# Hybrid decoder layer on one core: the first attention head's tensors loaded during the projections, the last down product's splits issued ahead of evictions, and the last output block computed in two halves

## Chip, cores and metric

The kernel runs on one core of one Trainium2 chip. The metric is the device time of one execution in microseconds. The kernel before was run three times; its time is the median of these runs. One further execution was recorded by the hardware profiler, and all durations quoted from a profile come from that one.

## The reference

The kernel computes one layer of a hybrid decoder for a sequence of 1024 tokens of width 1024, with 16 learned meta tokens put in front. All tensors are float32. Cut to what matters:

```python
h = concat([meta, x])                                  # 1040 x 1024
proj = rmsnorm(h, attn_norm_w) @ w_in                   # one projection, split by columns
o_gdn = gated_deltanet_group(...)                       # 4 heads of 128: short conv, chunked delta rule
# forgetting attention, 8 heads of 64, queries in blocks of 128, c = cumsum(log f):
sc = q[s:e] @ k[:e].T * scale + c[s:e, None] - c[None, :e]
p = softmax(where(causal, sc, MASK_VALUE))
o_fox = p @ v[:e]
h = h + concat([o_gdn, o_fox]) @ w_out
h = h + (silu(u @ w_gate) * (u @ w_up)) @ w_down        # u = rmsnorm(h, ffn_norm_w), d_ff = 2816
out = rmsnorm(h, final_norm_w)[16:]
```

## The kernel before

**Precision.** Every large product runs as three products of rounded operands: an operand is split into a high part (a cast by ScalarE, line 158) and a low part (a subtraction by VectorE, line 159), and high x high, high x low and low x high are summed in PSUM. The helper is `split` (line 157).

**Stages.** The layer is one long program: norm and projections; the delta-rule group's preparation and its scan over eight chunks of 128 tokens; attention over eight heads; the output projection; the feed-forward part; a final norm.

**The order on TensorE is written out by hand.** A small planner, `PeOrder` (line 43), keeps a modelled clock `od.t`. Chains of work are generators that yield the time at which their next step is due; whenever no chain is due, the planner takes the next matmul of a "fill". While the scan's chain runs (`scan`, line 692, one `chunk` of line 719 after another), the fill is `fox` (line 823): the attention group's projections, in the order v, k, q. `fox_proj` (line 672) works on blocks of 128 output columns, m = 0 to 3, in three chunks of some 342 to 348 tokens; each chunk's result is split into `fhl` (lines 687 and 688) and written to HBM (`q_d`, `k_d`, line 690). Afterwards the chain is `attention` (line 995), due `ATT0` = 9.0 modelled microseconds later (line 1077), and the fill is the delta-rule group's half of the output projection, `wout_gdn` (line 1057, tiles `wog`); six of its sixteen tiles are kept back for the stretch behind attention.

**The other engines and the DMA queue.** All DMAs named here are issued by SyncE (SP), in one queue. The order on VectorE, ScalarE, GpSimdE and SP is not written out: the framework's scheduler arranges it from the order of the program and a model of the times, and may move a load far ahead of its place in the program once the memory that it fills is free. `tc.issue_after(ins)` keeps instructions made inside it behind `ins` where they go to the same engine.

**The scan** loads for each chunk 1.75 MB in four DMAs (`ra`, `rb`, `rc`, `zt`, lines 722 to 728, two buffers each).

**Attention.** `att_head(h)` (line 885) issues eight DMAs for head h: `cr` (the cumulative gate, broadcast to 128 partitions), `sa` in two halves (q, high and low), `kk` in two halves (k, high and low), `vt` (v), and `vmt` twice (v of the meta tokens). Its tiles lie in the pool `al` (line 875), which is opened after the scan's pool `sp` is closed and so lies in memory that the scan used; each tag has two buffers, one for even and one for odd heads. Head 1's loads are kept behind the last write of `q_d` (line 1002). `scores` (line 903) makes two matmuls into one of two PSUM banks (lines 927 and 928), and VectorE adds the bias `bi` and takes a running minimum (line 930); ScalarE takes the exponential (line 935). `values` (line 950) transposes the probabilities and multiplies by v.

**The down product** comes as seven products p1, p6, p2, p7, p5, p4, p3 of half-sized blocks (`PH2`, line 1378), each of 11 operand pairs, in order of time. `down_ops` (line 1354) loads and splits a product's operands in three chunks of 4, 4 and 3 pairs; the three sets of buffers (`SETS`) are used in turn, so a product's third chunk takes the buffers of the third chunk of the product before. Each product but the last runs over four token blocks t inside each pair; the last, p3, runs block by block (line 1446), 33 matmuls of 512 columns each. `evict` (line 1414) adds a product from PSUM to its target; for p4 and p3 it then calls `final(u)` (line 1398), which for every block but 3 squares a row, takes the inverse root (line 205, on GpSimdE), multiplies (line 1040) and writes 512 KB to the output. The program has the operands' splits for the next product ahead of the evictions; the scheduler is free to mix them. For block 3, the last, `final` works in halves of 512 columns (lines 1404 to 1412).

Of the kernel before, what the change touches and what calls it, by code (L numbers as in the profile page):

```python
# [21 lines left out]
NT = S // P  # L22
GH = 4
FH = 8
DH = 64
DFF = 2816
NFF = DFF // P
EPS = 1e-6
# [3 lines left out]
GRP = 4  # L32
LV0 = (76.0, 119.0)
LAT = 0.4
ATT0 = 9.0
LEAD = 0.6
CO = 3.0
RES = 6
# [57 lines left out]
def tile_hymba_layer(ctx, tc, x, meta, attn_norm_w, w_in, conv_w, a_log, dt_bias, gdn_norm_w,  # L96
                     fgate_b, w_out, ffn_norm_w, w_gate, w_up, w_down, final_norm_w, out):
    nc = tc.nc
    x, out, w_in, conv_w = x[0], out[0], w_in[0], conv_w[0]
# [36 lines left out]
    mhalf = const.tile([P, 32], F32, name="mhalf")  # L136
# [10 lines left out]
    q_d = dram.tile([4, 2, P, S], F32, name="q_d")  # L147
# [6 lines left out]
    wraw = wrc.enter_context(tc.tile_pool(name="wraw", bufs=2, side="right"))  # L154
    wsp = wrc.enter_context(tc.tile_pool(name="wsp", bufs=4, side="right"))

    def split(dst_hi, dst_lo, src):
        cast = nc.scalar.copy(dst_hi, src)  # L158
        nc.vector.tensor_sub(dst_lo, src, dst_hi.bitcast(F32))  # L159
        return cast  # L160

    def load_w(parts, name):
# [40 lines left out]
    def inv_rms(dst, ssq, n, scale, tmp):  # L203
        nc.vector.tensor_scalar(tmp, ssq, scale, EPS, op0=ALU.mult, op1=ALU.add)
        nc.gpsimd.tensor_tensor(dst, tmp, mhalf[:tmp.shape[0], :n], op=ALU.pow)
# [12 lines left out]
    pre = ExitStack()  # L218
# [441 lines left out]
                                          w[1][k][:, :n]) for k in range(KT)], n / 2400)  # L660

    last = [None]

    fox_ws = [(GZ, 256, "z0"), (FV + 256, 264, "fv1"), (FV, 256, "fv0"), (FK, 256, "fk0"), (FK + 256, 256, "fk1"),
              (FQ, 256, "fq0"), (FQ + 256, 256, "fq1")]
# [6 lines left out]
    def fox_proj(dst, chunks, off, scale, nm):  # L672
        for b in range(2):
            w = fox_w.pop(0)
            for i in range(2):
                m = 2 * b + i
                for ci, (c0, n) in enumerate(chunks):
                    if (i, ci) == (0, 1):
                        fox_load()
                    acc = ps_mm(f"pj_{nm}{m}_{c0}")  # L680
                    yield from mm3g(acc[:, :n], [(w[0][k][:, P * i:P * i + P], w[1][k][:, P * i:P * i + P],
                                                  uh[:, k, c0:c0 + n], ul[:, k, c0:c0 + n])
                                                 for k in range(KT)], n / 2400)
                    od.on("act", n / 1200)
                    od.on("dve", n / 900)
                    hl = fp.tile([P, 2, 348], F32R, tag="fhl", name=f"fhl_{nm}{m}_{c0}")
                    nc.scalar.activation(hl[:, 0, :n], acc[:, :n], AF.Copy, scale=scale)
                    nc.vector.scalar_tensor_tensor(hl[:, 1, :n], acc[:, :n], scale, hl[:, 0, :n].bitcast(F32),
                                                   op0=ALU.mult, op1=ALU.subtract)
                    last[0] = nc.sync.dma_start(dst(m)[:, :, c0 - off:c0 - off + n], hl[:, :, :n].bitcast(F32))  # L690

    def scan():
        yield from meta_state()
# [168 lines left out]
    ogp = ogc.enter_context(tc.tile_pool(name="og", bufs=1))  # L862
    ogh = ogp.tile([P, GH, S], F32R, name="ogh")
    ogl = ogp.tile([P, GH, S], F32R, name="ogl")
    sp = scc.enter_context(tc.tile_pool(name="sp", bufs=1))
    cp = scc.enter_context(tc.tile_pool(name="cp", bufs=1, side="right"))
    od.add(scan(), od.t + 4.0, front=True)
# [4 lines left out]
    uctx.close()  # L872

    alc = ExitStack()
    al_ = alc.enter_context(tc.tile_pool(name="al", bufs=1))
    atc = ExitStack()
    ap_ = atc.enter_context(tc.tile_pool(name="ap", bufs=1, side="right"))
    ap2 = atc.enter_context(tc.tile_pool(name="ap2", bufs=1, side="right"))
    rsum = ap_.tile([P, FH, NT], F32, name="rsum")
    phm = ap2.tile([48, 512], F32R, name="phm")  # L880
    vmts = [al_.tile([48, P], F32R, name=f"vmt{i}") for i in range(2)]
    for z in [phm] + vmts:
        nc.gpsimd.memset(z.bitcast(F32), 0.0)

    def att_head(h):
        m, hb = h // 2, h % 2
        rows = slice(DH * hb, DH * hb + DH)
        kk = al_.tile([P, 2, T], F32R, tag="kk", bufs=2, name=f"kk_{h}")
        sa = al_.tile([P, S], F32R, tag="sa", bufs=2, name=f"sa_{h}")
        cr = al_.tile([P, T], F32, tag="cr", bufs=2, name=f"cr_{h}")  # L890
        nc.sync.dma_start(cr, c_d[h].partition_broadcast(P))
        for i in range(2):
            half = slice(DH * i, DH * i + DH)
            nc.sync.dma_start(sa[half].bitcast(F32), q_d[m, i, rows])
            nc.sync.dma_start(kk[half].bitcast(F32), k_d[m, rows])
        vt = al_.tile([P, NT, P], F32R, tag="vt", bufs=2, name=f"avt_{h}")
        nc.sync.dma_start(vt.bitcast(F32), v_d[h, NM:T].rearrange("(t p) d -> p t d", p=P))
        vmt = vmts[h % 2]
        for r in (0, 32):
            nc.sync.dma_start(vmt[r:r + NM].bitcast(F32), v_d[h, 0:NM])  # L900
        return m, rows, kk, sa, cr, vt, vmt

    def scores(h, g, hd, out):
        m, rows, kk, sa, cr, vt, vmt = hd
# [89 lines left out]

    def attention():
        groups = [(h, g) for h in range(FH) for g in range(NT // GRP)]
        hds, ptl, pos = {}, {}, [0.0]

        def score_stream():
            for i, (h, g) in enumerate(groups):  # L1000
                if h not in hds:
                    with tc.issue_after(last[0].ins) if h == 1 else nullcontext():
                        hds[h] = att_head(h)
                ptl[i] = []
                for n, rdy in enumerate(scores(h, g, hds[h], ptl[i])):
                    pos[0] = i + n / (5, 9)[g]
                    yield rdy
            pos[0] = 1e9

        ss = score_stream()  # L1010

        def ahead(x):
            while pos[0] < x:
                r = next(ss, None)
                if r is None:
                    return
                yield r

        yield from ahead(1.0)
        rot[0] = 0  # L1020
        for i, (h, g) in enumerate(groups):
            nt = GRP * (g + 1) + 1
            yield from ahead(i + 1.0)
            for k, rdy in enumerate(values(h, g, hds[h], ptl[i])):
                yield from ahead(i + 1.0 + LEAD + k / (2 * nt))
                yield rdy
        yield from av_step(0)
        rot[0] = 1
# [97 lines left out]
    rot[0] = 1  # L1126
    wo0c.close()
    alc.close()
    ogc.close()
    akc.close()  # L1130
    gplc.close()
# [179 lines left out]
    with tc.manual_schedule(engines={mybir.EngineType.PE}):  # L1311
# [76 lines left out]
        fnw = f3.tile([P, D], F32, name="fnw")  # L1388
        nc.sync.dma_start(fnw, final_norm_w.partition_broadcast(P))

        def down3(dst, op, t, first, i, cont):
            f, (ah, al), (wh, wl) = op
            c = slice(P * t, P * t + P)
            for n, (a, b) in enumerate(((ah, wh), (ah, wl), (al, wh))):
                nc.tensor.matmul(dst, a[:, f, c], b[:, f], start=(first and i == 0 and n == 0),  # L1395
                                 stop=(i == NF - 1 and n == 2), skip_group_check=cont)

        def final(t):
            y = f3.tile([P, D], F32, tag="y", bufs=3, name=f"y_{t}")
            if t != 3:  # L1400
                norm2(hs[t], fnw, y, f3, f"o{t}")
                nc.sync.dma_start(out[P * t:P * t + P], y)
                return
            sst = f3.tile([P, 6], F32, name="sst")
            halves = [lo_, hi_]
            for i, c in enumerate(halves):
                nc.scalar.activation(y[:, c], hs[t][:, c], AF.Square, accum_out=sst[:, i:i + 1])
            V.tensor_add(sst[:, 2:3], sst[:, 0:1], sst[:, 1:2])
            inv_rms(sst[:, 4:5], sst[:, 2:3], 1, 1.0 / D, sst[:, 3:4])
            for c in halves:  # L1410
                V.scalar_tensor_tensor(y[:, c], hs[t][:, c], sst[:, 4:5], fnw[:, c], op0=ALU.mult, op1=ALU.mult)
                nc.sync.dma_start(out[P * t:P * t + P, c], y[:, c])

        def evict(p, bk, t):
            u = t + 4
# [21 lines left out]
        for n, p in enumerate(PH2):  # L1437
            s = "y" if p in ("p6", "p7", "p4") else "x"
            first = p in ("p1", "p6", "p5", "p4")
            if first:  # L1440
                if s == "x":
                    sets[s] = [ps_s(f"x{p}{t}") for t in range(2)] + [ps_v(f"x{p}{t}") for t in range(2, 4)]
                else:
                    sets[s] = [ps_t(f"y{p}{t}") for t in range(3)] + [bank("mm", 1, f"y{p}3")]
            bk = sets[s]
            if p == "p3":
                for t in range(4):
                    for i, op in enumerate(ops):
                        down3(bk[t], op, t, first, i, not first)
                    evict(p, bk, t)  # L1450
                continue
            for i, op in enumerate(ops):
                for t in range(4):
                    down3(bk[t], op, t, first, i, not first)
            ops = down_ops(PH2[n + 1])
            for t in range(4):
                evict(p, bk, t)
        uoc.close()


# [24 lines left out]
```

## Time and profile before

| | |
|---|---|
| runs | 1362.46 us median of three (1359.22, 1362.46, 1362.53) |
| profiled execution | 1361.58 us, of which the span of the instructions 1359.8 us |
| mean granted TensorE clock | 0.986 |
| busy | PE 1308.9 us, VectorE 859.9, ScalarE 543.6, GpSimdE 424.0 |
| DMA | 242.11 MB, 178 GB/s in the mean |

A line of the timeline gives start and length in microseconds, the engine (PE is TensorE's matmuls, PEld its weight loads, DVE VectorE, ACT ScalarE, POOL GpSimdE, SPq the DMA issues of SyncE), the line of the program, the operation and the tiles written and read, with their shape; in brackets stands how long the engine was idle before it and who ended that. `x8` means that eight instructions were merged into one row, of which the chain's rows count weight loads too where these were on the chain. A line of the waits gives the waiting instruction, the one that ended the wait, the total in microseconds, the number of waits and the longest. A line of the stretches gives the busy time of each engine, and at its end the granted clock as a share of full speed, the share of time in which the DMA engines were busy, and GB/s. A line of DMA issues gives the number, the size of each, and the median time from issue to landing.

### The profile page before, as it was taken

The page shows a single profiled execution, that of the slowest core. Times are in us where ns is not written, and L with a number is a line of the kernel's source. Part 1 is how long each engine was busy: PE and PEld are TensorE (multiplying, and loading weights), DVE is VectorE, ACT ScalarE, POOL GpSimd, SP SyncE. Part 2 cuts the span into 40 slices and gives each one's busy share as a digit, 9 for nine tenths or more (in the row PEclk, how much of TensorE's full clock was granted, in tenths as well). Part 3 has the DMA queues.
Part 4 walks back from the last instruction along what each step waited for, and adds up shares of the span by engine and source line. Part 5 has one row for each costly group of instructions (what it writes and reads, how often), then busy time and mean ns, then how long its engine had stood idle before and what let it go on. Part 6 is the DMA issues. An engine that isn't in the chain of part 4 may idle for free.

```text
span 1359.8 us, 20162 instructions
## 1 busy us (share of the span) xinstructions
PE 1308.9 (96%) x7417; PEld 1137.2 (84%) x7417; DVE 859.9 (63%) x1505; ACT 543.6 (40%) x914; POOL 424.0 (31%) x422
## 2 busy tenths in 40 slices
PE   8999999999999899999778999999999999999997
PEld 7999999899999778887566878787888888888876
DVE  6565779657446578985677556666555566455653
ACT  6443543222223467872353233222223334333341
POOL 3111123211112256742432444433444443010300
PEclk9999999899999999999898999999999999999998
DMA  8131465784397898836526544445455556965522
GB/s 291 65 91 47 141 178 162 205 229 140 126 314 244 206 260 245 219 98 200 171 93 178 178 152 147 141 155 162 142 170 178 163 179 233 402 246 182 214 84 93
DMA packets 196201, 242.11 MB, mean 178 GB/s; under 512 B 18944, under 2 KB 146808, under 8 KB 192264
## 3 DMA queue, kind: packets, MB, share of 16 engines
q1 hardware_dynamic: 196104, 240.84, 56.6%
q8 instruction: 58, 0.95, 0.3%
q14 instruction: 39, 0.32, 0.1%
HBM read 161.62 MB, written 79.18 MB: 177 GB/s over the span
## 4 chain that ended last, share of the span: by engine, by line
PE 56%; DMA 15%; DVE 14%; POOL 7%; issue 5%; SPq 1%; ACT 1%; DVEq 0%; POOLq 0%; ACTq 0%
PE xp L1395 8%; PE yp L1395 6%; DMA raw_u<-in_w_up_dram 5%; PE pj_fk L199 3%; PE pj_fq L199 3%; DMA wt_p<-raw_d 3%; DMA raw_d<-in_w_down_dram 2%; PE wog L199 2%; PE pt L961 2%; DVE wl_u_p L159 2%; PE po L982 1%; PE pj_k L190 1%; PE pj_k L189 1%; PE pj_v L191 1%; PE pj_q L191 1%
## 5 line engine op out<-in xcount | busy, mean ns | idle before, releaser
L159 DVE TENSOR_TENSOR al_p<-ra_p,ah_p 128x2048 fp32r<-128x2048 f32 (+1 forms) x21 | 46.8, 2230 | 92.5 <-ACT ah_p L158 92.5
L914 POOL TENSOR_TENSOR bi<-ccol,cr 128x144 f32<-128x144 f32 (+7 forms) x60 | 70.7, 1182 | 55.5 <-DVE sm L930 51.2
L158 ACT CAST ah_p<-ra_p 128x2048 fp32r<-128x2048 f32 (+1 forms) x21 | 37.1, 1765 | 103.7 <-PE yp L1395 44.4
L1287 POOL TENSOR_TENSOR gz<-gz,uz 128x512 f32<-128x512 f32 x11 | 18.3, 1665 | 178.9 <-DVE uz L1282 149.8
L1395 PE MATMUL xp<-wl_p,ah_p 128*128 128x512 f32 x176 | 69.3, 394 | 1.8 <-DVE wl_p L159 1.8
L1395 PE MATMUL xp<-wh_p,al_p 128*128 128x512 f32 x176 | 69.1, 393 | 0.0
L1395 PE MATMUL xp<-wh_p,ah_p 128*128 128x512 f32 x176 | 69.0, 392 | 0.0
L158 ACT CAST wh_u_p<-raw_u 128x512 fp32r<-128x512 f32 x44 | 27.2, 620 | 74.6 <-DMA raw_u<-in_w_up_dram 23.7
L159 DVE TENSOR_TENSOR wl_u_p<-raw_u,wh_u_p 128x512 fp32r<-128x512 f32 x44 | 47.0, 1069 | 15.4 <-ACT wh_u_p L158 15.4
L935 ACT ACTIVATE pr<-pr,sm 128x144 f32<-128x144 f32 (+3 forms) x64 | 50.6, 791 | 13.7 <-DVE sm L930 12.1
L159 DVE TENSOR_TENSOR pl<-pt,ph 128x512 fp32r<-128x512 f32 (+1 forms) x96 | 51.5, 552 | 5.1 <-ACT ph L158 4.7
L159 DVE TENSOR_TENSOR wl_g_p<-raw_g,wh_g_p 128x512 fp32r<-128x512 f32 x44 | 38.7, 881 | 23.4 <-ACT wh_g_p L158 23.4
L158 ACT CAST ph<-pt 128x512 fp32r<-128x512 f32 (+1 forms) x96 | 45.2, 473 | 20.3 <-PE pt L961 18.3
L158 ACT CAST wh_g_p<-raw_g 128x512 fp32r<-128x512 f32 x44 | 27.1, 619 | 63.7 <-PE ub L1237 42.0
L1223 DVE TENSOR_TENSOR ws_g<-raw_g,raw_g 128x512 f32<-128x512 f32 x11 | 7.6, 692 | 69.6 <-DMA raw_g<-in_w_gate_dram 69.6
L1395 PE MATMUL yp<-wh_p,ah_p 128*128 128x512 f32 x132 | 51.3, 389 | 0.0
L1395 PE MATMUL yp<-wl_p,ah_p 128*128 128x512 f32 x132 | 51.3, 389 | 0.0
L1395 PE MATMUL yp<-wh_p,al_p 128*128 128x512 f32 x132 | 51.3, 389 | 0.0
L159 DVE TENSOR_TENSOR wl_p<-rw_p,wh_p 128x2048 fp32r<-128x2048 f32 (+1 forms) x21 | 46.5, 2213 | 4.7 <-ACT wh_p L158 4.7
L961 PE MATMUL pt<-ident,pr 128*128 128x128 f32 x288 | 48.2, 276 | 0.0
L927 PE MATMUL sc<-kk,sa 128*128 128x144 f32 (+6 forms) x112 | 40.7, 364 | 4.9 <-issue 3.3
L930 DVE CUSTOM_DVE_ANT_0 pr<-sc,bi 128x144 f32<-128x144 f32 (+3 forms) x64 | 31.5, 492 | 15.7 <-PE sc L928 11.8
(591 smaller groups left out, 4521.7 us busy)
## 6 DMA issues: line engine op xcount, KB each, us to landing
ra_p<-ao_p SPq DMA_DIRECT2D x14, 1024.0 KB, 6.4
raw_g<-in_w_gate_dram SPq DMA_DIRECT2D x23, 512.0 KB, 4.8
raw_u<-in_w_up_dram SPq DMA_DIRECT2D x23, 512.0 KB, 5.4
raw_d<-in_w_down_dram SPq DMA_DIRECT2D x22, 512.0 KB, 4.6
wt_p<-raw_d SPq DMA_DIRECT2D x33, 256.0 KB, 2.4
kk<-k_d SPq DMA_DIRECT2D x16, 520.0 KB, 10.0
rw_p<-wt_p SPq DMA_DIRECT2D x8, 1024.0 KB, 6.1
rw_p<-in_w_down_dram SPq DMA_DIRECT2D x6, 1024.0 KB
```

Of the source, the lines that this page charges most:

```text
L158: cast = nc.scalar.copy(dst_hi, src)
L159: nc.vector.tensor_sub(dst_lo, src, dst_hi.bitcast(F32))
L189: nc.tensor.matmul(dst, lh, rh, start=(i == 0), stop=False)
L191: nc.tensor.matmul(dst, ll, rh, start=False, stop=(i == n - 1))
L199: nc.tensor.matmul(dst, a, b, start=first, stop=last)
L914: nc.gpsimd.tensor_tensor(bi[:, :n], ccol[:, h, j:j + 1].broadcast_to([P, n]), cr[:, :n], op=ALU.subtract)
L927: nc.tensor.matmul(sc[:, :b - a], sa[:, q0:q0 + P], kk[:, 0, a:b], start=True, stop=False)
L930: V.tensor_tensor_reduce(out=pr[:, a:b], in0=sc[:, :b - a], in1=bi[:, a:b], scale=1.0, scalar=3e38 if i == 0 else sm[:, i - 1:i], op0=ALU. ...
L935: nc.scalar.activation(pr[:, :n], pr[:, :n], AF.Exp, bias=sm[:, np_ - 1:np_], scale=-1.0, accum_out=rsum[:, h, j:j + 1])
L961: nc.tensor.transpose(pt[:rows_k, P * j:P * j + P], pts[j][0][:, c0:c0 + rows_k], ident)
L1287: G.tensor_tensor(gs[d], gs[d], us[d], op=ALU.mult)
L1395: nc.tensor.matmul(dst, a[:, f, c], b[:, f], start=(first and i == 0 and n == 0), stop=(i == NF - 1 and n == 2), skip_group_check=cont)
```

## The change

There are three edits.

1. **Head 0's loads.** `att_head` and the zeroing of `vmt` are moved ahead of the projections' code. Instead of one pool with two buffers there are two pools with one buffer each: `al0`, for even heads, is opened before the scan's pool `sp` and so lies below it, and `al`, for odd heads, is opened where the old pool was. `fox_proj` calls `att_head(0)` once the block m = 1 of q has been issued, while the scan is under way. `ATT0` falls from 9.0 to 2.0.
2. **The last splits.** `split` remembers its last pair of instructions. For p4 the evictions (with the final norm of blocks 4 to 7 in them) are kept behind the last split of p3's operands on both engines.
3. **The last block.** p3's block 3 runs as two halves of 256 columns, 33 matmuls each, in the same PSUM bank. `last_part(0)` does what can be done for the first 512 columns beforehand (the square and its sum, the product with the norm's weight), `last_part(1)` the columns 512 to 767 between the halves, `last_part(2)` the rest. `final(3)` then has one combination of the sums, the inverse root, one product of 256 columns that takes both factors, and two scalings (ScalarE 512 columns, VectorE 256), and writes the upper half first.

```diff
-ATT0 = 9.0
+ATT0 = 2.0
...
+    tail = [None]
+
     def split(dst_hi, dst_lo, src):
         cast = nc.scalar.copy(dst_hi, src)
-        nc.vector.tensor_sub(dst_lo, src, dst_hi.bitcast(F32))
+        tail[0] = (cast, nc.vector.tensor_sub(dst_lo, src, dst_hi.bitcast(F32)))
         return cast
...
+    alp, vmts, hds = [], [], {}
+
+    def al_pool(pool):
+        alp.append(pool)
+        vmts.append(pool.tile([48, P], F32R, name=f"vmt{len(vmts)}"))
+        nc.gpsimd.memset(vmts[-1].bitcast(F32), 0.0)
+
+    def att_head(h):
+        m, hb = h // 2, h % 2
+        rows = slice(DH * hb, DH * hb + DH)
+        al_ = alp[hb]
+        kk = al_.tile([P, 2, T], F32R, tag="kk", name=f"kk_{h}")
+        sa = al_.tile([P, S], F32R, tag="sa", name=f"sa_{h}")
+        cr = al_.tile([P, T], F32, tag="cr", name=f"cr_{h}")
...
                     last[0] = nc.sync.dma_start(dst(m)[:, :, c0 - off:c0 - off + n], hl[:, :, :n].bitcast(F32))
+                if (nm, m) == ("fq", 1):
+                    hds[0] = att_head(0)
...
     ogl = ogp.tile([P, GH, S], F32R, name="ogl")
+    al0c = ExitStack()
+    al_pool(al0c.enter_context(tc.tile_pool(name="al0", bufs=1)))
     sp = scc.enter_context(tc.tile_pool(name="sp", bufs=1))
...
-    al_ = alc.enter_context(tc.tile_pool(name="al", bufs=1))
+    al_pool(alc.enter_context(tc.tile_pool(name="al", bufs=1)))
...
-        def down3(dst, op, t, first, i, cont):
+        def down3(dst, op, t, first, i, cont, n_=slice(0, H)):
...
-                nc.tensor.matmul(dst, a[:, f, c], b[:, f], start=(first and i == 0 and n == 0),
+                nc.tensor.matmul(dst[:, n_], a[:, f, c], b[:, f, n_], start=(first and i == 0 and n == 0),
...
+            pre, h = fin
+            V.scalar_tensor_tensor(pre[:, 4:5], pre[:, 2:3], 1.0 / D, pre[:, 3:4], op0=ALU.mult, op1=ALU.add)
+            G.tensor_tensor(pre[:, 5:6], pre[:, 4:5], mhalf[:, 0:1], op=ALU.pow)
+            r = pre[:, 5:6]
+            V.scalar_tensor_tensor(y[:, 768:], h[:, 768:], r, fnw[:, 768:], op0=ALU.mult, op1=ALU.mult)
+            nc.scalar.activation(y[:, lo_], hw[:, lo_], AF.Copy, scale=r)
+            V.tensor_scalar(y[:, 512:768], hw[:, 512:768], r, None, op0=ALU.mult)
+            nc.sync.dma_start(out[P * t:P * t + P, hi_], y[:, hi_])
+            nc.sync.dma_start(out[P * t:P * t + P, lo_], y[:, lo_])
...
+        def last_part(i):
+
+            pre, h = fin
+            c = (lo_, slice(512, 768), slice(768, D))[i]
+            if i:
+                V.tensor_add(h[:, c], bk[3][:, c.start - 512:c.stop - 512], h[:, c])
+            nc.scalar.activation(sq[:, c], h[:, c], AF.Square, accum_out=pre[:, i:i + 1])
+            if i < 2:
+                V.tensor_mul(hw[:, c], h[:, c], fnw[:, c])
+            if i == 1:
+                V.tensor_add(pre[:, 0:1], pre[:, 0:1], pre[:, 1:2])
+                V.tensor_scalar(pre[:, 3:4], pre[:, 0:1], 1.0 / D, EPS, op0=ALU.mult, op1=ALU.add)
...
             if p == "p3":
-                for t in range(4):
+                for t in range(3):
...
+                last_part(0)
+                for q in range(2):
+                    for i, op in enumerate(ops):
+                        down3(bk[3], op, 3, first, i, not first, slice(256 * q, 256 * q + 256))
+                    last_part(1 + q)
+                final(3)
                 continue
...
             ops = down_ops(PH2[n + 1])
-            for t in range(4):
-                evict(p, bk, t)
+            late = [tc.issue_after(x.ins) for x in tail[0]] if p == "p4" else [nullcontext()] * 2
+            with late[0], late[1]:
+                for t in range(4):
+                    evict(p, bk, t)
```

More of the change, by code (lines that the diff above doesn't have):

```diff
@@ L662, in tile_hymba_layer @@
     last = [None]
+    alp, vmts, hds = [], [], {}
[10 more added lines that the diff above has]
+        cr = al_.tile([P, T], F32, tag="cr", name=f"cr_{h}")
+        nc.sync.dma_start(cr, c_d[h].partition_broadcast(P))
+        for i in range(2):
+            half = slice(DH * i, DH * i + DH)
+            nc.sync.dma_start(sa[half].bitcast(F32), q_d[m, i, rows])
+            nc.sync.dma_start(kk[half].bitcast(F32), k_d[m, rows])
+        vt = al_.tile([P, NT, P], F32R, tag="vt", name=f"avt_{h}")
+        nc.sync.dma_start(vt.bitcast(F32), v_d[h, NM:T].rearrange("(t p) d -> p t d", p=P))
+        vmt = vmts[hb]
+        for r in (0, 32):
+            nc.sync.dma_start(vmt[r:r + NM].bitcast(F32), v_d[h, 0:NM])
+        return m, rows, kk, sa, cr, vt, vmt
     fox_ws = [(GZ, 256, "z0"), (FV + 256, 264, "fv1"), (FV, 256, "fv0"), (FK, 256, "fk0"), (FK + 256, 256, "fk1"),
@@ L880, in tile_hymba_layer @@
     phm = ap2.tile([48, 512], F32R, name="phm")
[L881 to L901, printed above, removed]
+    nc.gpsimd.memset(phm.bitcast(F32), 0.0)
     def scores(h, g, hd, out):
@@ L996, in attention @@
         groups = [(h, g) for h in range(FH) for g in range(NT // GRP)]
-        hds, ptl, pos = {}, {}, [0.0]
+        ptl, pos = {}, [0.0]
         def score_stream():
@@ L1128, in tile_hymba_layer @@
     alc.close()
+    al0c.close()
     ogc.close()
@@ L1403, in final @@
                 return
[L1404 to L1412, printed above, removed]
+            pre, h = fin
[7 more added lines that the diff above has]
+            nc.sync.dma_start(out[P * t:P * t + P, lo_], y[:, lo_])
+        fin = [f3.tile([P, 6], F32, name="sst"), hs[3]]
+        hw, sq = (f3.tile([P, D], F32, name=n) for n in ("hw", "sqj"))
+        def last_part(i):
[9 more added lines that the diff above has]
+                V.tensor_scalar(pre[:, 3:4], pre[:, 0:1], 1.0 / D, EPS, op0=ALU.mult, op1=ALU.add)
         def evict(p, bk, t):
```

## The prediction

> **What bounds the kernel now.** I read the busy shares first, then who the matmul engine waited for, then its clock by stretches, then the timelines around the places that the change touches.
>
> ```profile
> span 1359.8 us, 20162 instructions
> PE 1308.9 (96%) x7417; PEld 1137.2 (84%) x7417; DVE 859.9 (63%) x1505; ACT 543.6 (40%) x914; POOL 424.0 (31%) x422
> ```
> ```profile
> PE rbt L1096 <- POOL rx L1093: 15.1, 3, 9.3
> ...
> PE xp L1395 <- DVE wl_p L159: 1.8, 1, 1.8
> ```
> ```profile
> 459.23 0.40 PE L199 MATMUL wog<-whi_wo,ogl 128*128 128x512 f32 x1
> 462.95 0.30 PE L927 MATMUL sc<-kk,sa 128*128 128x144 f32 x1 [3.33 <-issue]
> ...
> 477.77 0.30 PE L927 MATMUL sc<-kk,sa 128*128 128x144 f32 x1 [1.15 <-DMA kk<-k_d]
> ```
>
> PE is busy for 1308.9 of 1359.8 us, so an edit pays only where it removes a gap of PE, a stretch of slow PE clock, or time behind the last matmul. The largest wait (15.1, on the way from attention to the feed-forward part) is not touched. Three others are: 3.33 us before the first attention score, 1.15 before the second head's scores, and 1.8 in the last down product. Two of them have a sequel in the clock (the third number from the end is the granted clock, after the busy times):
>
> ```profile
> 462.00:464.00 2.00, 1.04 (x7) 0.98 (x8) 0.47 (x3) 0.12 (x1) 0.00 (x0) 1.00 1.13 307
> 478.00:482.00 4.00, 4.00 (x18) 3.26 (x17) 1.43 (x8) 1.49 (x7) 2.81 (x4) 0.57 1.07 392
> 1327.00:1333.00 6.00, 6.00 (x21) 4.74 (x21) 3.46 (x5) 1.15 (x2) 1.48 (x3) 0.72 0.45 178
> ```
>
> Right behind the 1.15 us gap the clock is near half: 4 x 0.43 = 1.72 us of matmul time lost. Behind the 1.8 us gap: 6 x 0.28 = 1.68. Behind the 3.33 us gap nothing. I take the two losses as sequels of their gaps, because each begins within about 1 us of one.
>
> **Part by part: attention's start.** Now head 0's loads wait for the scan's memory and are issued from 449.18 on:
>
> ```profile
> 449.18 0.32 SPq L891 DMA_DIRECT2D cr<-c_d  x1
> 449.55 0.43 SPq L690 DMA_DIRECT2D q_d<-fhl_fq  x1
> 450.02 0.52 SPq L894 DMA_DIRECT2D sa<-q_d  x1
> ...
> 451.87 0.73 SPq L895 DMA_DIRECT2D kk<-k_d  x1
> ...
> 453.33 3.70 SPq L900 DMA_DIRECT2D vmt<-v_d  x2
> ...
> 457.62 0.41 SPq L690 DMA_DIRECT2D q_d<-fhl_fq  x1
> ```
> ```profile
> L199 PE MATMUL wog<-whi_wo,ogh x64: 388/392/628, 451.9 to 628.2; 128*128 128x512 f32 x64
> ```
> ```profile
> 454.29 0.50 DVE L688 SCALAR_TENSOR_TENSOR fhl_fq<-pj_fq,fhl_fq 128x340 fp32r<-128x340 f32 x1
> ```
>
> The fill (wog) starts at 451.9. With ATT0 = 2.0 scores may start at 453.9. The fill that ran before them is not lost: it lies between scores later, so only the idle 3.33 us can go. DVE cannot read a score before it is through with fhl_fq at 454.79, and only two score banks exist, so up to 0.9 us stays, less what fill covers: I take 0.4 left, a gain of 2.9.
>
> Head 1 must follow the last q_d write, as now. That write waited at 457.62 behind head 0's loads on SP; with those gone it goes out at about 454.85, and head 1's cr at 455.3. The second kk came 2.69 after cr in head 0 (451.87 - 449.18), so 458.0, and it lands 10.0 later (row below): 468.0. It is needed as far behind the first score as now, 477.77 - 1.15 - 462.95 = 13.67: at 453.9 + 0.4 + 13.67 = 468.0. So the 1.15 us gap about closes; I leave 0.3, a gain of 0.85, and let the halved clock behind it go, 1.72. Bounds: all 1.15 gone, or as much left as now.
>
> The price: head 0's eight DMAs move into the scan, whose loads share SP.
>
> ```profile
> 399.73 0.42 SPq L724 DMA_DIRECT2D rb<-rec_d  x1
> ```
> ```profile
> 411.20 0.89 PE pvn L742 x8
> ```
> ```profile
> DMA packets 12202, 25.06 MB, mean 251 GB/s; under 512 B 998, under 2 KB 6598, under 8 KB 12036
> ...
> rb<-rec_d SPq DMA_DIRECT2D x8, 512.0 KB, 5.7
> ...
> kk<-k_d SPq DMA_DIRECT2D x4, 520.0 KB, 10.0
> ...
> cr<-c_d SPq DMA_DIRECT2D x2, 520.0 KB
> sa<-q_d SPq DMA_DIRECT2D x4, 256.0 KB
> avt<-v_d SPq DMA_DIRECT2D x2, 512.0 KB
> ```
>
> The fourth chunk's rb is issued at 399.73, lands 5.7 later and is needed at 411.20 (the fourth pvn): 5.8 us to spare. Head 0's issues held SP from 449.18 to 457.03, less q_d's 0.43: 7.4. Their bytes, 520 + 2 x 256 + 2 x 520 + 512 KB = 2.58 MB, take 10.3 us at 251 GB/s. So the scan, and PE with it (its order is written out), loses 0 (the issues fall between the scan's), 7.4 - 5.8 = 1.6, or 10.3 - 5.8 = 4.5. I take 1.6: the issue rows are the operation itself. The zeroing of vmt moves with them, two memsets on POOL, whose cost I put at nothing: the scan's products on POOL behind them have the same 5.8 to spare.
>
> Sum of this part: -2.9 - 0.85 - 1.72 + 1.6 = -3.9.
>
> **The last splits.**
>
> ```profile
> 1289.34 21.55 PE yp L1395 x95
> ```
> ```profile
> 1292.34 1.75 DVE L159 TENSOR_TENSOR wl_p<-rw_p,wh_p 128x1536 fp32r<-128x1536 f32 x1
> ...
> 1317.26 2.80 DVE L1430 TENSOR_TENSOR hs<-yp,hs 128x512 f32<-128x512 f32 x4
> ...
> 1320.85 2.48 DVE L1040 SCALAR_TENSOR_TENSOR y<-hs,st_o,fnw 128x1024 f32<-128x1024 f32 x2 [0.42 <-POOL st_o L205]
> ...
> 1324.91 1.75 DVE L159 TENSOR_TENSOR wl_p<-rw_p,wh_p 128x1536 fp32r<-128x1536 f32 x1
> ```
>
> Ninety-five matmuls in 21.55 us are 0.227 each. p4 starts at 1289.34 and has 132: p3 starts at 1319.3. Its third chunk's w split is done at 1326.66 now, behind two of final's products. In the same place one phase earlier nothing stood ahead, and it was done at 1294.09, 4.75 behind the phase's start. So 1324.05; p3's first block needs it for its 26th matmul, 25 x 0.227 = 5.7 in, at 1325.0. The wait of 1.8 goes with 0.9 to spare, and with it 1.68 of clock. What now waits: p4's adds (2.80) and final's products (4 x 1.24) and behind them p3's first eviction, on DVE till about 1333. No matmul needs those banks again, and block 3 starts only at 1319.3 + 3 x 33 x 0.227 = 1341.8, 9 us later; that block covers it, and without it the backlog would stand ahead of the last outputs. Sum -3.5; if the clock is not tied to the gap, -1.8.
>
> **The last block in halves.**
>
> ```profile
> 208.73 0.28 PE L199 MATMUL z<-whi_z,uh 128*128 128x256 f32 x1
> ...
> 212.98 0.28 PE L199 MATMUL z<-whi_z,uh 128*128 128x256 f32 x1
> ```
> ```profile
> 478.57 0.42 DVE L159 TENSOR_TENSOR pl<-pt,ph 128x256 fp32r<-128x256 f32 x1
> ```
> ```profile
> 1352.90 0.69 DVE L1433 TENSOR_TENSOR hs<-xp,hs 128x512 f32<-128x512 f32 x1 [3.27 <-PE xp L1395]
> 1354.38 0.16 DVE L1408 TENSOR_TENSOR sst<-sst 128x1 f32<-128x1 f32 x1 [0.79 <-ACT y L1407]
> 1354.58 0.15 DVE L204 TENSOR_SCALAR sst<-sst 128x1 f32<-128x1 f32 x1
> 1355.39 1.42 DVE L1411 SCALAR_TENSOR_TENSOR y<-hs,sst,fnw 128x512 f32<-128x512 f32 x2 [0.66 <-POOL sst L205]
> ```
> ```profile
> PE gd L1237 <- DVE gz L1282: 4.9, 6, 1.8
> ```
>
> Thirty-six steps in 4.25 us are 0.118 a matmul of 256 columns; 66 x 0.118 - 33 x 0.227 = +0.3. Both halves lie in one PSUM bank, and the first is read by DVE before the second is written. Whether PE waits for that read no row shows; nearest is gd, where a matmul waits for DVE's read of its bank, 0.82 each. Ends 0 and 0.82; I take 0.6, the 0.42 add and two handovers; behind that wait stand on PE only the second half's 33 matmuls, and behind them the tail.
>
> The Trainium skill, "PSUM — Partial Sum Buffer", section on bank collisions, says to guard a bank as a whole, not by address; by it the wait is there, without it the sum is 0.6 lower.
>
> Behind the last matmul: the add falls from 0.69 to 0.42, its square (256 columns instead of 512) by about as much, 0.27, the addition of the partial sums (0.20 start to start) goes, and 1.42 of products becomes two of about 0.4 beside ACT's. That is 0.27 + 0.27 + 0.20 + 0.6 = 1.3 up to the first output's issue. The second output now follows it on SP by an issue (0.4 to 0.5), so I take 0.9, ends 0.3 and 1.3. Sum 0.3 + 0.6 - 0.9 = 0.
>
> **Sum.** -3.9 - 3.5 + 0 = -7.4. The profiled execution took 1361.58: 1354.2. The median of the runs, 1362.46, is 0.9 above it and their lowest, 1359.22, 2.4 below; between 1354.2 and 1355.1 I predict 1354.6. About 0.3%, 4.1 us, is what a measurement of this kernel can tell from no change: faster means below 1358.4.
>
> **Rivals.** (1) The scan is starved: 4.5 instead of 1.6 and a halved stretch as behind the other gaps, +2.9 + 1.7: 1359.2. For it: 251 GB/s over the whole stretch; against: the 5.8 to spare. Chance 0.14. (2) The wait moves to head 1: its gap stays as now with its slow clock, +0.85 + 1.72: 1357.2. For it: the estimate left no margin. Chance 0.18. (3) The slow clock isn't tied to these gaps and comes elsewhere: +3.4: 1358.0; for it, 3.33 us of idleness brought none. Chance 0.14. The Trainium skill, "TensorE: Matmul & The Clock Gate" (What's actually happening), has the clock halve after an idle window of about 3.4 us; by it neither short gap would do it, and the trace speaks against it with 0.57 behind 1.15 us. (4) Slower: head 0's loads sit on SP waiting for a write ahead of them, and hold the scan's loads for longer than they take themselves. The gains without the scan's price are 9.0, so it decides above 5.8 + 9.0 = 14.8 us of hold (18.9 for 0.3%); issue to first score, 462.95 - 449.18 = 13.8, and another rb's 5.7 would make 19.5: 1354.6 - 1.6 + 13.7 = 1366.7. Against: sa was issued at 450.02, with a q_d write in flight, so only the rows it reads count. Chance 0.04.
>
> **Numbers.** Forecast 0.50. Its own range: at best -3.33 - 1.15 - 1.72 - 3.48 + 0.3 - 1.3 = -10.7, 1350.9; above it the rivals up to 1359.4 come in, which leaves out (4) and part of (1). Faster: 0.48 of the forecast, 0.16 of (2), 0.09 of (3), 0.04 of (1): 0.77. Same 0.19, slower 0.04.
>
> **Right or wrong.** In the profile after: no idle before the first score; a gap under 0.5 before head 1's; no wait on wl_p in the last phase and clock 1.00 there; a new PE wait of some 0.6 on hs in the last block; waits on ra, rb or rc in the scan would show (1) or (4).

## The result, and the profile after

The kernel after is slower. The forecast was 1354.6 us, in a range of 1350.9 to 1359.4.

| | before | after |
|---|---|---|
| runs beside each other, median of four | 1362.49 us (1359.22 to 1362.62) | 1370.41 us (1367.1 to 1370.7) |
| ratio, 95% interval | | 1.0058 [1.0037, 1.0080] |
| profiled execution, span | 1361.58, 1359.8 | 1370.55, 1368.6 |
| mean granted TensorE clock | 0.986 | 0.98 |

Head of the page, after; then the waits of PE after (total, number, longest):

```profile
span 1368.6 us, 20237 instructions
PE 1312.5 (96%) x7450; PEld 1143.9 (84%) x7450; DVE 862.1 (63%) x1509; ACT 545.4 (40%) x917; POOL 425.8 (31%) x422
```
```profile
PE rbt L1107 <- POOL rx L1104: 13.9, 3, 8.8
PE sc L938 <- DMA h_d<-ht: 5.5, 1, 5.5
...
PE p L762 <- DMA ra<-rec_d: 2.5, 1, 2.5
...
PE xp L1407 <- DVE hs L1434: 0.7, 1, 0.7
```

The wait on `wl_p` (1.8) and the 3.33 us before the first score are gone, and the bank wait on `hs` is there. In the stages that the change touches, two waits stand out: 2.5 us inside the scan, where the same product `p` had waited for nothing before, and 5.5 before head 1's scores in place of 1.15. Both show in PE's timeline, and both are followed by a slow clock in the stretches behind them, 4.85 x 0.34 = 1.65 us and 5.75 x 0.36 = 2.07 lost. The product `p` before, then after; then after alone:

```profile
393.81 1.16 PE L733 MATMUL p<-s,ra 128*128 128x128 f32 x8
```
```profile
399.15 2.04 PE L762 MATMUL p<-s,ra 128*128 128x128 f32 x8 [2.54 <-DMA ra<-rec_d]
```
```profile
461.06 0.23 PE L938 MATMUL sc<-kk,sa 128*128 128x144 f32 x1
```
```profile
480.25 0.46 PE L938 MATMUL sc<-kk,sa 128*128 128x144 f32 x1 [5.52 <-DMA h_d<-ht]
```
```profile
399.15:404.00 4.85, 4.85 (x25) 4.85 (x26) 2.05 (x7) 0.76 (x1) 0.57 (x1) 0.66 1.02 281
480.25:486.00 5.75, 5.75 (x25) 4.97 (x26) 2.80 (x12) 3.26 (x9) 3.44 (x5) 0.64 1.08 246
1329.00:1345.00 16.00, 16.00 (x72) 13.28 (x71) 10.65 (x15) 7.47 (x11) 2.96 (x4) 1.00 0.17 67
```

In p3, the last of the down products, the clock is whole (1.00, the last row). To see which stage pays, I cut each profiled execution at the first and last matmuls of named tiles: **q** is the projection of q beside the scan (`pj_fq`, first to last), **attention** runs from there to the last value product (`po`), **down product** is the whole of it, p1 to p3, from the first matmul into `xp` to the last, **end** from there to the end of the span; **rest** is all else.

| profiled execution | q | attention | down product | end | rest | span |
|---|---|---|---|---|---|---|
| before | 98.2 | 158.5 | 212.9 | 7.3 | 882.9 | 1359.8 |
| after | 102.6 | 162.1 | 210.7 | 6.6 | 886.6 | 1368.6 |
| tail_only | 98.3 | 157.0 | 210.7 | 6.6 | 887.9 | 1360.5 |
| head_only | 103.6 | 160.7 | 211.3 | 7.2 | 887.2 | 1370.0 |
| att9 | 104.1 | 152.0 | 210.6 | 7.5 | 884.4 | 1358.6 |
| head1_first | 103.0 | 161.2 | 210.7 | 6.8 | 888.3 | 1370.0 |
| no_ht | 101.2 | 158.5 | 210.7 | 6.9 | 885.8 | 1363.1 |
| quiet9 | 98.3 | 153.7 | 210.7 | 6.8 | 885.3 | 1354.8 |
| quiet5 | 98.3 | 156.0 | 210.7 | 6.5 | 885.0 | 1356.5 |
| quiet2 | 98.3 | 164.3 | 210.7 | 6.5 | 885.0 | 1364.8 |
| quiet12 | 98.3 | 154.5 | 210.7 | 6.6 | 881.6 | 1351.7 |
| quiet9_head_only | 98.3 | 153.1 | 212.9 | 7.3 | 884.0 | 1355.6 |
| before_att2 | 98.3 | 162.0 | 212.9 | 7.3 | 881.7 | 1362.2 |

After against before: +4.4 in q, +3.6 in attention, -2.9 in the down product and the end, together +5.1; and +3.7 in the rest. The rest scatters between 881.6 and 888.3 over the thirteen, so its 3.7 is no effect of the change that this study can show. The edits to the tail gained; both losses belong to head 0's loads and `ATT0`.

The attention can be taken apart further, since it has the same matmuls in both (907 and 908 records). The stretch before, then after; the third number is PE's busy time:

```profile
451.60:610.10 158.50, 152.77 (x907) 126.55 (x905) 126.98 (x360) 116.83 (x265) 88.90 (x126) 0.99 0.80 213
```
```profile
458.50:620.60 162.10, 153.15 (x908) 127.69 (x906) 129.45 (x360) 116.73 (x265) 89.27 (x126) 0.97 0.76 199
```

PE's idle time there is 5.73 before (3.33 and 1.15 the most of it) and 8.95 after: 5.52, and 2.31 at a place that had no wait before, some 90 us into the attention:

```profile
548.03 0.49 PE L988 MATMUL po<-phm,vmt 48*128 48x512 f32 x1 [2.31 <-DVE phm L161]
```
```profile
544.31 2.54 DVE L161 TENSOR_TENSOR wlo_wo<-raw_wo,whi_wo 128x1024 fp32r<-128x1024 f32 x1
546.78 0.48 DVE L941 CUSTOM_DVE_ANT_0 pr<-sc,bi,sm 128x264 f32<-128x264 f32 x1
547.19 0.08 DVE L941 DVE_READ_ACCUMULATOR2_ANT sm<- 128x1 f32 x1
547.29 0.68 DVE L161 TENSOR_TENSOR phm<-pt_-1_6239,phm 16x512 fp32r<-16x512 f32 x1
```

There the split of a weight tile (2.54 us on DVE) stands ahead of the probabilities that PE waits for. It is itself long: the split before it took 1.23 us (at 538.87, GpSimdE idle beside it), and beside this one GpSimdE is at work all the time. Whether that is the reason, no run here shows. With fewer fill matmuls ahead of the scores the fill's weights are needed later: their last load is issued at 546.9 instead of 522.9.

### The profile page after: what moved, and what is told of

It is laid out like the page before. It is cut to its first block, busy times and chain, and to the rows that moved or that the text cites. A ratio compares the mean times of both kernels' runs of the same rounds, so it can differ in the third digit from the quotient of the medians.

```text
span 1368.6 us, 20237 instructions
## 1 busy us (share of the span) xinstructions
PE 1312.5 (96%) x7450; PEld 1143.9 (84%) x7450; DVE 862.1 (63%) x1509; ACT 545.4 (40%) x917; POOL 425.8 (31%) x422
## 4 chain that ended last, share of the span: by engine, by line
PE 55%; DMA 15%; DVE 13%; POOL 7%; issue 5%; SPq 1%; ACT 1%; POOLq 0%; DVEq 0%; ACTq 0%
PE xp L1407 9%; PE yp L1407 7%; DMA raw_u<-in_w_up_dram 5%; PE pj_fk L201 3%; PE pj_fq L201 3%; PE wog L201 3%; DMA raw_d<-in_w_down_dram 2%; DMA wt_p<-raw_d 2%; PE pt L972 2%; DVE wl_u_p L161 2%; DMA rkr<-rk_d 1%; PE po L993 1%; PE sc L938 1%; PE pj_k L192 1%; PE pj_k L191 1%
## 5 line engine op out<-in xcount | busy, mean ns | idle before, releaser
L1407 PE MATMUL xp<-wh_p,ah_p 128*128 128x512 f32 (+1 forms) x187 | 70.5, 377 | 0.7 <-DVE hs L1434 0.7
L1407 PE MATMUL xp<-wl_p,ah_p 128*128 128x512 f32 (+1 forms) x187 | 70.4, 377 | 0.0
L1407 PE MATMUL xp<-wh_p,al_p 128*128 128x512 f32 (+1 forms) x187 | 70.4, 376 | 0.0
L1407 PEld LDWEIGHTS xp<-wh_p,ah_p 128*128 128x128 f32 x187 | 35.2, 188 | 7.3 <-DVE hs L1434 0.9
```

The lines of the kernel that those rows point to most:

```text
L1407: nc.tensor.matmul(dst[:, n_], a[:, f, c], b[:, f, n_], start=(first and i == 0 and n == 0), stop=(i == NF - 1 and n == 2), skip_group_che ...
```

## What stood on SP

The scan first. SP's issues from 384 to 395, before and then after:

```profile
384.82 0.37 SPq L690 DMA_DIRECT2D q_d<-fhl_fq  x1
385.43 3.76 SPq L722 DMA_DIRECT2D ra<-rec_d  x2
```
```profile
384.10 1.61 SPq L688 DMA_DIRECT2D vmt<-v_d  x2
387.79 0.38 SPq L717 DMA_DIRECT2D q_d<-fhl_fq  x1
391.28 0.34 SPq L679 DMA_DIRECT2D cr<-c_d  x1
391.71 0.38 SPq L751 DMA_DIRECT2D ra<-rec_d  x1
392.58 1.72 SPq L682 DMA_DIRECT2D sa<-q_d  x2
```

Before, the next `ra` goes out at 385.43 and its product `p` runs at 393.81 without a wait. After, `ra` stands behind head 0's `vmt` and `cr`, goes out at 391.71 and is waited for until 399.15. SP issues nothing from 388.17 to 391.28 with `cr` next in its queue; `cr` reads `c_d`, whose last write ended its issue at 383.51 and must land first. SP's own waits between 388.0 and 391.5 name just that:

```profile
SPq L679 <- DMA c_d<-crow: 3.0, 1, 3.0
```

Then the start of attention. SP after, beginning when the scan's memory comes free:

```profile
456.03 0.33 SPq L1074 DMA_DIRECT2D ht<-in_x_dram  x1
456.42 0.43 SPq L717 DMA_DIRECT2D q_d<-fhl_fq  x1
456.88 2.12 SPq L1074 DMA_DIRECT2D ht<-in_x_dram  x4
459.05 2.67 SPq L172 DMA_DIRECT2D raw_wo<-in_w_out_dram  x2
462.36 0.37 SPq L717 DMA_DIRECT2D q_d<-fhl_fq  x1
462.77 0.46 SPq L679 DMA_DIRECT2D cr<-c_d  x1
...
465.00 0.45 SPq L683 DMA_DIRECT2D kk<-k_d  x1
...
467.00 0.45 SPq L683 DMA_DIRECT2D kk<-k_d  x1
```

Head 0's eight issues are gone from here, but seven others have come in ahead of head 1's `cr`: five residual tiles `ht` and two weight tiles `raw_wo`. Before, the same five `ht` loads were made at the very start of the kernel (rows of `ht` before, here to 20 us; count, median issue time in ns, first and last start):

```profile
L1063 SPq DMA_DIRECT2D ht<-in_x_dram x5: 328/328/462, 7.8 to 13.3; - x5
```

They could be, because their memory lay above the scan's pool and was free from the beginning. With `al0` put below `sp`, the scan's pool is about 21 KB a partition higher and covers that memory until the scan is over. Added up from the tiles of the program, in bytes of a partition above the pool `og`: `al0` takes 21,184; the scan's 38,912 then end at 60,096 in place of 38,912; and the pool of `ht` begins at 42,368 in both. I had not worked out these addresses before I predicted.

## The experiments

**Theory A**: the loss is the scan's late `ra`, and a start 7 us earlier (`ATT0` 2.0) that asks for head 1's loads, and the loads now beside them, sooner than they can land. **Rivals**: the tail's edits cost the time; only the order on SP behind the scan matters; the late `ht` loads alone are it. "Before" is the kernel before, timed beside each. Kernels of one group shared its runs: first tail_only to head1_first, then quiet9 to no_ht, then the last three.

**tail_only** undoes the first edit and keeps the other two:

```diff
-ATT0 = 2.0
+ATT0 = 9.0
-                if (nm, m) == ("fq", 1):
-                    hds[0] = att_head(0)
...
-    al_pool(al0c.enter_context(tc.tile_pool(name="al0", bufs=1)))
```

> The changed kernel without its first part: attention's pool, head 0's loads and ATT0 = 9.0 as before, the last splits and the last block in halves as changed. Theory A (the loss comes from the moved loads alone): the tail still gains what the changed kernel's trace shows behind the start of the down product, about 3 us, so 1359 to 1360 and nothing lost anywhere else. Rival B (the tail's edits cost as much as they gain): 1362 to 1363.

Measured 1361.15 us, ratio 0.9988 [0.9967, 1.0009]. The tail's edits cost nothing that shows, so the loss isn't theirs. A small gain is likely, but the interval holds 1 and does not decide between the two expectations.

**head_only** is the kernel before with the first edit alone (edits 2 and 3 taken back).

> The first part alone: the two pools, head 0's loads during the projections and ATT0 = 2.0; the tail as before. Theory A: the whole loss and the 1.8 us wait in the last down product with its slow clock, 1370.4 + 3 = 1373 to 1374. Rival B: about 1370, as the changed kernel.

Measured 1370.12, ratio 1.0054 [1.0028, 1.0079]: the whole loss. The 3 us more that theory A expected did not show; the down product and the end are 1.2 us longer than in the kernel after. Its profile has both new waits (2.9 on `ra`, 4.7 before head 1). It also has the old wait of 1.8 in p3, and behind it the clock stayed whole:

```profile
1338.60 0.50 PE L1407 MATMUL xp<-wl_p,ah_p 128*128 128x512 f32 x1 [1.80 <-DVE st_o L206]
```
```profile
1339.00:1345.00 6.00, 6.00 (x28) 4.96 (x27) 3.58 (x5) 1.15 (x2) 1.37 (x3) 1.00 0.45 178
```

**att9** is the kernel after with one number back:

```diff
-ATT0 = 2.0
+ATT0 = 9.0
```

> The changed kernel with ATT0 = 9.0 instead of 2.0. Theory A (head 1's loads come late, because five ht loads that could be issued at the kernel's start now wait for the scan's memory and stand ahead of them): head 1's tensors land as late as in the changed kernel, but are needed up to 7 us later, so the 5.5 us gap closes nearly and the scan's 2.5 us gap stays: 1362 to 1366. Rival C (it is the scan alone that loses): the gap before head 1 is as wide as with 2.0 and the time stays at 1369 to 1371.

Measured 1360.72, ratio 0.9980 [0.9958, 1.0003], a little better than the 1362 to 1366 of theory A. The attention falls from 162.1 to 152.0, below the 158.5 of before, while the scan's price stays (q 104.1, 2.5 on `ra`). So the earlier start is the larger loss, and head 0's early loads are worth something without it.

**head1_first** is the kernel after with head 1's loads issued ahead of `ht` and `raw_wo`:

```diff
     nc.gpsimd.memset(phm.bitcast(F32), 0.0)
+    hds[1] = att_head(1)
```

> The changed kernel, ATT0 = 2.0, with head 1's loads put into the program ahead of the output projection's, and not held behind the last write of q_d; so on SP they stand ahead of the five ht loads and the two weight loads. Theory A: head 1's gap falls from 5.5 to under 2 us, and with the slow clock behind it 4 to 7 us are won: 1363 to 1367; the scan's gap stays. Rival D (ATT0 = 2.0 itself is wrong: scores come before their inputs whatever the order): the gap moves to the ht loads or to another head, and the time stays at 1369 to 1372.

Measured 1371.34, ratio 1.0059 [1.0022, 1.0096]. The gap before head 1's scores is gone, and one as long stands elsewhere:

```profile
472.94 0.80 PE L201 MATMUL wog<-whi_wo,ogh 128*128 128x512 f32 x1 [4.75 <-DVE ht L1078]
```

The fill's bank is only emptied by adding into `ht`; with `ht` last in the queue the fill stops instead. Order alone gives nothing: what comes second is late. Theory A as I had put it for this run fell; the loads of both kinds together are too many for the time.

**quiet9, quiet5, quiet2** keep head 0's loads off the scan. They are called once the scan's last load has been issued, and `ATT0` is 9.0, 5.5 and 2.0:

```diff
-                if (nm, m) == ("fq", 1):
-                    hds[0] = att_head(0)
+                    if (nm, m, ci) == ("fq", 3, 0):
+                        with tc.issue_after(lastz[0].ins):
+                            hds[0] = att_head(0)
...
-        nc.sync.dma_start(zt, rec_d[t, :, 7])
+        lastz[0] = nc.sync.dma_start(zt, rec_d[t, :, 7])
```

> All of the change, but head 0's loads held on SP behind the scan's very last load (zt of chunk 7), where the DMA engines stand idle before the scan's end, and ATT0 = 9.0. Theory E (early loads do win at attention's start; the change lost it by placing them where the scan's loads were already late, and by ATT0): no ra wait in the scan, 98 us for the q projection instead of 104, attention as short as with ATT0 = 9.0 in the earlier run (152 us from the last projection to the last value product); so 1.0 - 0.0020 - 5/1360 = 0.994 of the kernel before, about 1353 where that takes 1360.5. Rival F (the scan's loss comes from where the scan's own tiles and loads lie in memory and on SP, not from head 0's bytes): the ra wait and the 104 us stay, ratio 0.998.

> The same placing with ATT0 = 5.5. Theory E: between the two, the wait before head 1 about 2 us, ratio 0.995 to 1.000. If the gain were only a matter of starting scores early, this would beat 9.0.

> The same placing of head 0's loads with the change's ATT0 = 2.0. Theory E: the scan's loss goes, the loss inside attention (head 1's and the output projection's loads needed 7 us sooner than they can land) stays: about 5 us under the changed kernel, ratio 1.001 to 1.003. Rival G (ATT0 only hurts because the scan has left the DMA queue late): as fast as with 9.0, ratio 0.994.

Measured 1357.89, ratio 0.9971 [0.9953, 0.9989]; 1359.84, 0.9982 [0.9966, 0.9998]; 1366.12, 1.0018 [0.9997, 1.0038]. In all three q takes 98.3 as before and no `p` waits for `ra`, which shows the scan's price to be a matter of place; rival F fell. In the whole times that price shows with `ATT0` 2.0 (1.0058 in the old place, 1.0018 here) and hardly with 9.0 (0.9980 of att9, 0.9971 here), where att9's attention is 1.7 us shorter and the intervals leave open how much of it arrives. The 0.994 expected of quiet9 was too much: its interval ends at 0.9953. SP in quiet9:

```profile
438.40 0.32 SPq L758 DMA_DIRECT2D zt<-rec_d  x1
438.77 0.43 SPq L679 DMA_DIRECT2D cr<-c_d  x1
...
442.46 2.78 SPq L688 DMA_DIRECT2D vmt<-v_d  x2
```

What is left is `ATT0`: attention 153.7, 156.0 and 164.3. With 2.0 the first score is early (455.63) and head 1's wait is longer than in the kernel after; with 9.0 no wait on a load is left in the attention, and the clock is whole there. The row of the wait in quiet2, then the whole attention in quiet2 and in quiet9:

```profile
476.51 0.46 PE L939 MATMUL sc<-kk,sa 128*128 128x144 f32 x1 [6.41 <-DMA h_d<-ht]
```
```profile
453.10:617.40 164.30, 153.74 (x908) 127.86 (x905) 129.48 (x360) 116.51 (x265) 89.19 (x126) 0.96 0.77 201
```
```profile
452.40:606.10 153.70, 150.94 (x907) 125.63 (x905) 127.30 (x360) 116.86 (x265) 89.84 (x126) 1.00 0.78 214
```

The same matmuls take 153.74 us of PE and 10.56 of idle time in quiet2, 150.94 and 2.76 in quiet9: some 8 us are waits and some 3 slow clock.

**no_ht** is the kernel after with the five tiles zeroed; it leaves out the residual for them:

```diff
-        nc.sync.dma_start(ht, x[cols, nbc])
+        if nb == 0 and tt < 5:
+            nc.gpsimd.memset(ht, 0.0)
+        else:
+            nc.sync.dma_start(ht, x[cols, nbc])
```

> The changed kernel, ATT0 = 2.0, with the residual left out for the first five output-projection tiles: their ht is zeroed on GpSimdE instead of loaded, so 1.28 MB are not in the queue ahead of head 1's loads. Theory A (the ht loads, which now wait for the scan's memory, are what head 1 waits for): head 1's gap falls from 5.5 to about 5.5 - 1.28 MB / 0.25 MB per us = 0.4, and with the slow clock behind it 5 to 8 us are won, ratio about 1.000. Rival H (the loads after the scan come too late for ATT0 = 2.0 even so, the two weight loads and head 1's own 2.6 MB being enough): gap 3 us or more, ratio 1.003 or more.

Measured 1368.13, ratio 1.0029 [1.0002, 1.0057], between the two expectations. Head 1's wait falls from 5.5 to 2.6, not to nothing:

```profile
476.36 0.30 PE L938 MATMUL sc<-kk,sa 128*128 128x144 f32 x1 [2.62 <-DMA kk<-k_d]
```

So the displaced `ht` loads are about half of that wait (2.9 of 5.5), and the rest stands without them.

**quiet12** is quiet9 with `ATT0 = 12.5`.

> The quiet9 kernel with ATT0 = 12.5 instead of 9.0. Theory A (head 1's loads, the five residual loads and the two weight loads need about 20 us behind the scan, and a start that asks for them sooner idles): at 9.0 no wait on a load was left in the attention, so 3.5 us more buy nothing; ratio to the kernel before 0.996 to 0.999, within 0.2% of quiet9's 0.9971. Rival B (the later the better): 0.995 or lower, attention at least 2 us shorter than quiet9's 153.7 us.

Measured 1357.27, ratio 0.9971 [0.9954, 0.9989], the same as quiet9; attention 154.5. Past 9.0 nothing is left to gain, and rival B fell.

**before_att2** is the kernel before with `ATT0 = 2.0`.

> The kernel before with ATT0 = 2.0 and nothing else. Theory A (the start is bound by the loads' landing, not by ATT0): head 0's scores cannot start before about 462 us, so with fewer fill matmuls written ahead of them the idle before the first score grows from 3.33 to about 7 to 10 us and head 1's gap stays near 1; ratio 1.003 to 1.006. Rival B (ATT0 = 2.0 harms only together with the moved pool and its late residual loads): ratio 0.999 to 1.001.

Measured 1365.85, ratio 1.0037 [1.0024, 1.0049]. The first score comes when it did before, after a longer wait:

```profile
462.22 0.46 PE L927 MATMUL sc<-kk,sa 128*128 128x144 f32 x1 [8.66 <-issue]
```

It stands 11.1 us behind the issue of head 0's last `kk` in both (451.87 to 462.95 before, 451.11 to 462.22 here). The row names no releaser ("issue"), but in the kernels with head 0's loads early this gap is gone, so the start is set by the loads' landing. The lower number only takes away fill that stood ahead of it: 8.66 idle instead of 3.33. Head 1's gap, which I expected to stay near 1, is gone, since its loads had the same time and its scores came no sooner.

**quiet9_head_only** is quiet9 with edits 2 and 3 taken back.

> The quiet9 kernel with the last phase and last block as before. Theory A (the parts add): 0.9971 plus the 0.0012 that the tail's edits gave alone: 0.998, interval below 1. Rival B (the tail's edits carried most of quiet9's gain): 0.999 to 1.001.

Measured 1358.11, ratio 0.9981 [0.9967, 0.9996]: head 0's early loads alone are a gain, and the rest of quiet9's is what the tail gives, within the intervals.

quiet9 and quiet12 beat both kernels, by 0.29% [0.11, 0.47] for quiet9. Their stages add up to more than that in the profiles (quiet9: -4.8 in attention, -2.7 in the down product and the end, 7.5 us against 4.0 by the ratio). The attention of one order of work gave 158.5 and 157.0 (before, tail_only), which accounts for 1.5 of it; the rest is not settled.

## Why the prediction was wrong

**First score: right.** The 3.33 us are gone, and the first score comes 2.6 us behind the last q matmul (461.06 against 458.5; forecast 454.3 against 451.6, 2.7).

**Head 1: the step that failed.** I put its landing and its need both at 468.0 and left 0.3 of gap. Counted from the start of the last q matmul, in us:

| | forecast | after | quiet2 | no_ht |
|---|---|---|---|---|
| head 1's `cr` issued | 3.7 | 4.3 | 5.5 | 4.4 |
| last `kk`, behind `cr` | 2.7 | 4.2 | 4.1 | 3.3 |
| from there to the end of the wait | 10.0 | 13.3 | 13.8 | 12.3 |
| landed | 16.4 | 21.8 | 23.4 | 20.0 |
| needed | 16.4 | 16.2 | 17.0 | 17.3 |

The need was right to 0.2 and the issue of `cr` to 0.6; the later `kk` issue (1.5) and the landing (3.3) make 5.4 of late arrival with that, against the 5.5 measured. (The row names a write of `h_d` as the last releaser; the scores read only `kk` and `sa`, so 13.3 bounds the landing from above.) The estimate carried SP's freed time over as free; it was taken up by loads that the moved pool had pushed behind the scan. And it took head 0's 2.69 between the two issues and the median landing of four loads, 10.0. The kernel before had shown both for this very load, and longer: head 1's last `kk` was issued 5.64 behind its `cr` there, and landed 11.6 later:

```profile
460.38 0.34 SPq L891 DMA_DIRECT2D cr<-c_d  x1
```
```profile
466.02 0.45 SPq L895 DMA_DIRECT2D kk<-k_d  x1
```

With these, the forecast's own sum is 455.3 + 5.64 + 11.6 = 472.5, which is 4.5 too late. So most of the 5.5 could be read off before the change, and not all of it belongs to the displaced loads: in no_ht, without the five residual tiles, 12.3 remain. An estimate without margin on a transfer was priced as if it had one: 0.3 us, and the bound that I gave ("as much left as now") reached to 1.15 only. Rival (2) had the place and a price too small: a missed landing costs the whole shortfall, not the old gap.

**The second cost of the lower `ATT0`**, 2.31 us behind a weight split with a piece of halved clock after it (some 1.7 us lost), was in no term: I had looked at the fill's matmuls, which lose nothing by standing later, and not at the splits that come with them. It is in every kernel with 2.0 and early loads for head 0 (2.3 to 3.0 us) and not in quiet9, att9 or before; quiet5 and quiet12 have 1.9 and 1.8 of it, so it is no matter of that number alone.

**The clock behind head 1's gap** was not freed: 2.07 us are lost there now, in place of 1.72.

**The scan: mis-sized.** Forecast +1.6 within 0 to 4.5, measured +4.4 in after and 4.8 to 5.9 in the others with the same place (head_only, att9, head1_first; no_ht 3.0). I had priced the hold by `rb`, which had 5.8 to spare, at SP's issue times only. It was `ra`, 6.3 later (391.71 against 385.43) where q starts only 2.5 later (355.9 against 353.4), so 3.8 late in relation to the work around it. Head 0's `vmt` and `cr` held it, with 3.1 us of an idle SP between. That is the mechanism of rival (4); the price, 2.54 + 1.65 = 4.2 of wait and clock, is below rival (1)'s 4.5 + 1.7 and far below rival (4)'s 13.7.

**The last splits: right in the gap, and the clock's part was not certain.** Forecast -3.5 with the last block's +0.9 behind it, so -2.6 in the down product; measured 212.9 to 210.7, -2.2. All nine executions without the wait have 210.6 or 210.7; of four with it three have 212.9 and one 211.3, the one whose clock stayed whole. So rival (3) has a share: the 1.68 is a sequel of that gap in most executions and not in all.

**The last block: right.** Bank wait 0.69 against 0.6:

```profile
1358.04 0.39 PE L1407 MATMUL xp<-wh_p,ah_p 128*128 128x256 f32 x1 [0.69 <-DVE hs L1434]
```

The end fell from 7.3 to 6.6, 0.7 against 0.9. The Trainium skill's advice ("PSUM — Partial Sum Buffer", bank collisions) to guard by bank agrees with that row: the second half waits for the read of the first half's columns.

**The sum.** Forecast -3.9 for attention's start and the scan, measured +4.4 + 3.6 = +8.0; forecast -3.5 for the tail, measured -2.9 in the profiles, and -1.6 [-4.5, +1.2] by the ratio of tail_only. Of the 11.9 between -3.9 and +8.0, head 1's gap is 5.2, its clock 2.1, the scan 2.8, and the second cost 2.3 + 1.7, less 0.4 at the first score. That is 13.7, or 1.8 more than the stages lost; where these 1.8 came back is not settled.

## What to carry to other kernels

Before a load is moved earlier, work out where its memory lies: a pool put below another shifts everything above it, and loads that the scheduler had made early, because their memory was free, become late without a line of theirs being changed. An earlier start is worth only as much as the second item's loads allow; where the estimate says "just in time", price the miss by the landing times under full DMA load, and keep the start where the fill covers it. Take a load's price from rows of that load, not from its sibling's: here head 0's spacing and a median hid 4.5 us. A load that waits for a write belongs behind the other loads of a shared queue, here behind the scan's last: the same eight loads cost 4.4 us of the scan's stage in the one place and nothing in the other.

## What the hardware showed that I had not expected

The halved clock comes in pieces of about 3.4 us (at half speed 0.70 over 5.64 us, the row below, is 2 x 0.30 x 5.64 = 3.4; 0.57 over 4.00 and 0.72 over 6.00 in the kernel before come to the same), and the length of a gap does not tell whether one follows. A gap of 1.15 us (before, head 1) had one behind it, and 1.8 in p3 in three executions of four; the 3.33 before the first score had none, while the same gap in tail_only, 3.38 us in the same order of work, had one:

```profile
465.36:471.00 5.64, 5.64 (x22) 4.89 (x23) 2.92 (x11) 3.21 (x9) 2.30 (x4) 0.70 1.09 330
```

The Trainium skill ("TensorE: Matmul & The Clock Gate", What's actually happening) says that activity is judged in windows of about 3.4 us that run freely, beside the program. That agrees with the length of the pieces and with a like gap being followed by one in one execution and not in another. Its "idle window" does not agree with 1.15 us of idleness being enough, so here a gap was priced best by how often a piece followed it, not by a threshold.
